# Conditioning rows as whole 2048-wide tiles of 1 MB, and a new share-out of them over the groups of a two-layer trunk

## The chip, the cores and the metric

The kernel runs on one core of one Trainium2 chip. The metric is the device time of one execution in microseconds (us). A core has TensorE (PE, matmuls; PEld is its weight load), VectorE (DVE), ScalarE (ACT), GpSimd (POOL) and SyncE (SP), each with an in-order queue of its own, and 16 DMA engines that move data between HBM and SBUF. Matmul results land in PSUM.

## The reference

A sequence of 256 tokens with 2048 features passes two layers. Each layer is a token mixer followed by a squared-ReLU MLP with 8192 hidden features. Layer 0 mixes with an attention of three branches (compressed, selected, window), layer 1 with differential attention. Every sub-layer is conditioned by a vector `c`: six vectors of 2048 per layer come from one large matrix-vector product, and they scale, shift and gate.

```
mod_all = einsum('bd,lde->lbe', silu(c), ada_w) + ada_b        # 2 layers x 6 vectors x 2048
for i in range(2):
    sh1, sc1, g1, sh2, sc2, g2 = split(mod_all[i], 6)
    h = rms_norm(x, attn_norm_g[i]) * (1 + sc1) + sh1
    x = x + g1 * mixer_i(h)                                    # ends in an output projection 2048 x 2048
    h = rms_norm(x, mlp_norm_g[i]) * (1 + sc2) + sh2
    x = x + g2 * (square(relu(h @ mlp_w1[i])) @ mlp_w2[i])
```

All data are float32. `ada_w` alone is 201 MB, and all weights together some 600 MB, each byte of which is read once.

## The kernel before

**Weight groups.** All large products are done in groups. A group is four steps `u`; each step loads two weight tiles of 128 x 1024 float32 (512 KB, tag `raw`, five buffers) from SyncE's queue, and `split` turns each into a rounded part `wH` (ACT) and the remainder `wL` (DVE), with three buffers each, so that TensorE can use its fp32r format: three matmuls per product (line 239 to 241, or 231 to 233 where the activations are the stationary side). `ws_group` runs a group with weights as the stationary side into two PSUM tiles; four such PSUM tiles exist.

**The conditioning rows.** One conditioning vector is 16 rows of 128 x 2048: 128 outputs on the partitions, 2048 inputs along the row. A row is loaded and multiplied with the broadcast `silu(c)` (`cbc`) in one DVE instruction that also sums it up (`accum_out`). The 32 rows of the first two vectors are done in stage 1 by `ada_row`, whole, beside the first weights (`ws`, tiles `psc`, `psv`). The other 160 rows wait in a list `ada_q` in the order layer 0 vectors 2 to 5, layer 1 vectors 0 to 5. `ada_tile` does one of them as two halves of 1024, 512 KB each, in a pool of three buffers (`ADAB`).

Each step of a group ends in `ada_step(rate)`, which issues rows from the list at a given rate:

```
ada_credit[0] += rate
while ada_credit[0] >= 1.0 - 1e-9 and ada_pos[0] < len(ada_q):
    l, vec, kt = ada_q[ada_pos[0]]
    ada_tile(l, vec, kt)
    ada_pos[0] += 1
    ada_credit[0] -= 1.0
```

`ada_until(l, vec)` issues what is still missing up to a vector, and sets the credit to zero for each row that it forces. `ada_vec` adds the halves and the bias once a vector's 16 rows are traced.

**Order.** The instructions are traced in program order and a scheduler gives each engine a fixed queue before the kernel runs. A conditioning load is kept behind the last weight load traced before it (`issue_after(last_load[0])`), and its DVE instruction has its priority lowered by 150 (`AOFF`). A load waits in SyncE's queue until its buffer is free, with all later loads behind it.

**Stages.** After stage 1 come the key groups k0 and k1 (weights `wi`), whose steps also do a part of the compression MLP (weights `cw1`, tile `hidps`) at rate `RA` = 1.3; four query groups with attention at `RB` = 1.2; the output projection `nwo` at `RC` = 1.6. `w_out_phase` runs the projection's first two column groups to three quarters early, finishes them, and then runs groups 2 and 3. Behind group 2 `ready()` needs vectors 3 and 4, and twelve of the sixteen scalings of the next input `z` follow; behind group 3 the last four. Then `mlp` begins with `pair`: two groups (tiles `m_z`) that run on the unnormalised `z` while the norm's statistics and the modulated input `hn` are still being made; these two have no `ada_step`. Groups nb 2 and nb 3 of chunk 0 run at `CR[2]`, `CR[3]`, the first `w2` group at `CR[4]`, and `ada_until(0, 5)` stands ahead of its `residual`, which needs vector 5. All other MLP groups (108 steps) run at `MR0`. Layer 1 does the same: a pair `dvz`, `dkz`, ten groups dq, dk, dv with attention at `DR`, the projection `dwo` at `DR`, an MLP.

Of the kernel before, what the change touches and what calls it, by code (L numbers as in the profile page):

```python
# [11 lines left out]
F32 = mybir.dt.float32  # L12
# [4 lines left out]
ALU = mybir.AluOpType  # L17
PSUM = bass.MemoryType.PSUM

P = 128  # L20
T = 256
TT = T // P
D = 2048
KT = D // P
DFF = 8192
DEPTH = 2
# [7 lines left out]
AOFF = 150  # L34
PMA = ((0, 1), (0, 2), (1, 1))

RA, RB, RC = 1.3, 1.2, 1.6
DR = 0.3
MR0 = 0.8
MR1 = 0.3  # L40
CR = (0, 0, 1, 1, 1)
NEARLY = 2
ACT_SET = "natural_log_exp_and_others"
DH = 128
# [13 lines left out]
NVEC = 6 * KT  # L58
# [17 lines left out]
def emit(ctx, tc, nc, a):  # L76
# [5 lines left out]
    adap = pool("adap", bufs=ADAB)  # L82
# [3 lines left out]
    sm = pool("sm", bufs=2)  # L86
# [10 lines left out]
    def tt(out, in0, in1, op):  # L97
        V.tensor_tensor(out=out, in0=in0, in1=in1, op=op)  # L98

    def stt(out, in0, scalar, in1, op0, op1, **kw):  # L100
        V.scalar_tensor_tensor(out, in0, scalar, in1, op0=op0, op1=op1, **kw)  # L101
# [10 lines left out]
    def sc(name):  # L112
        return scp.tile([P, 512], F32, tag="sc", name=name)
# [18 lines left out]
    cbc = cst.tile([P, D], F32, name="cbc")  # L132
# [6 lines left out]
    for q in range(4):  # L139
        ps = sc("cps")  # L140
# [6 lines left out]
    adaacc = {}  # L147
    mod = cst.tile([P, DEPTH, 6, KT], F32, name="mod")
    bT = smallT[:, SM_B:SM_B + DEPTH * NVEC].rearrange("p (l v) -> p l v", l=DEPTH)

    last_load = [None]

    def acc_tile(l, vec):
        if (l, vec) not in adaacc:
            adaacc[l, vec] = sm.tile([P, KT, 2], F32, tag="adaacc", name="adaacc", bufs=3)
        return adaacc[l, vec]

    def ada_tile(l, vec, kt):
        e = vec * KT + kt
        for j in range(2):  # L160
            r = adap.tile([P, 1024], F32, tag="ada", name="adaraw")
            if last_load[0] is not None:
                with tc.issue_after(last_load[0]):
                    nc.sync.dma_start(r, a["adaT"][l, e, j])
            else:
                nc.sync.dma_start(r, a["adaT"][l, e, j])
            acc = acc_tile(l, vec)[:, kt, j:j + 1]
            with tc.high_priority(offset=-AOFF if (l, vec) > (0, 1) else 0):
                stt(r, r, 1.0, cbc[:, j * 1024:(j + 1) * 1024], ALU.mult, ALU.mult, accum_out=acc)


    def ada_row(vec, kt):
        r = actp.tile([P, D], F32, tag="act", name="adarow")
        nc.sync.dma_start(r.rearrange("p (j d) -> p j d", j=2),
                          a["adaT"][0, vec * KT + kt].rearrange("j p d -> p j d"))
        acc = acc_tile(0, vec)[:, kt, 0:1]
        stt(r, r, 1.0, cbc, ALU.mult, ALU.mult, accum_out=acc)
        return acc

    def ada_vec(l, vec):  # L180
        e = vec * KT
        m = mod[:, l, vec, :]
        tt(m, acc_tile(l, vec)[:, :, 0], acc_tile(l, vec)[:, :, 1], ALU.add)
        tt(m, m, bT[:, l, e:e + KT], ALU.add)

    ada_q = []
    for l in range(DEPTH):
# [8 lines left out]
    def ada_step(rate):  # L196
# [6 lines that stand above are left out]
            if kt == KT - 1:  # L203
                ada_vec(l, vec)

    def ada_until(l, vec):
        while ada_pos[0] < len(ada_q) and ada_q[ada_pos[0]][:2] <= (l, vec):
            ada_credit[0] = 0.0
            ada_step(1.0)
# [33 lines left out]
    def mm_tile(name):  # L243
        return mmp.tile([P, 512], F32, tag="mm", name=name)

    def xs_group(name, srcs, tiles, rate, extra=None):
        ps = [mm_tile(f"{name}{t}") for t in range(TT)]
        for u in range(4):
            for hf in range(2):
                H, L = split(load(srcs(u)[hf]))  # L250
                for j in range(2):
                    kt = u * 4 + hf * 2 + j
                    for t in range(TT):
                        xs_mm(ps[t], tiles, kt, t, H, L, j * 512, 512, kt == 0, kt == KT - 1)
            ada_step(rate)
            if extra is not None:
                extra(u)
        return ps

    def ws_part(ps, srcs, tiles, rate, us, extra=None):  # L260
        for u in us:
            for hf in range(2):
                H, L = split(load(srcs(u)[hf]))
                for n, j in [(n, j) for n in range(4) for j in range(2)] if u * 2 + hf == 7 else \
                        [(n, j) for j in range(2) for n in range(4)]:
                        kt = u * 4 + hf * 2 + j
                        ws_mm(ps[n // 2][:, (n % 2) * T:(n % 2 + 1) * T], tiles, kt, H, L,
                              j * 512 + n * P, kt == 0 and n % 2 == 0, kt == KT - 1 and n % 2 == 1)
            ada_step(rate)
            if extra is not None:  # L270
                extra(u)

    def ws_group(name, srcs, tiles, rate):
        ps = [mm_tile(f"{name}{t}") for t in range(2)]
        ws_part(ps, srcs, tiles, rate, range(4))
        return ps
# [223 lines left out]
    def residual(tn, ps, nb, l, vec, stats):  # L500
        for n in range(4):
            kt = nb * 4 + n
            stt(xT[:, kt, :], ps[n // 2][:, (n % 2) * T:(n % 2 + 1) * T], mod[:, l, vec, kt:kt + 1],
                xT[:, kt, :], ALU.mult, ALU.add)
            if stats:
                if nb == 3:
                    tn.scale(kt)
                tn.st.add(kt)
        if stats and nb == 2:
            tn.ready()  # L510
            for kt in range(12):
                tn.scale(kt)
# [3 lines left out]
    def pop(more=False):  # L516
        for _ in range(1 + more):
            if pend:
                pend.pop(0)()

    def w_out_phase(name, src, tiles, l, rate, extra=None):
        tn = Turn(l, 1)
        early = [[mm_tile(f"{name}{nb}_{t}") for t in range(2)] for nb in range(NEARLY)]
        for nb in range(NEARLY):
            ws_part(early[nb], lambda u: src[nb, u], tiles, rate, range(3), extra and (lambda u: extra()))
        while pend:
            pop()
        ada_until(l, 2)
        for nb in range(4):
            if nb < NEARLY:  # L530
                ps = early[nb]
                ws_part(ps, lambda u: src[nb, u], tiles, rate, range(3, 4))
            else:
                ps = ws_group(f"{name}{nb}_", lambda u: src[nb, u], tiles, rate)
            residual(tn, ps, nb, l, 2, True)
        return tn

# [69 lines left out]
    for kt in range(KT):  # L607
        acc = ada_row(1, kt)
        stt(Amod[:, 0, 0, kt:kt + 1], acc, b1[:, kt:kt + 1], ag[:, 0, kt:kt + 1], ALU.add, ALU.mult)
        acc = ada_row(0, kt)  # L610
# [4 lines left out]
        f, la = kt == 0, kt == KT - 1  # L615
# [8 lines left out]
    for i in range(2):  # L624
        V.memset(kcT[i][:, :, 256:272], 0.0)
        for b in range(2):
            src = ps_c[i][b].rearrange("p (g t) -> p g t", g=2)
# [93 lines left out]
    def part(i, hp):  # L721
        def f(u):
            cmp_part(i, hp, u)
            pop()
        return f

    hidk = cmp_start(0)
    ps = xs_group("k0_", lambda u: blocks[0, u], h, RA, part(0, hidk))
    pend += [k_block(tab_ks, (128, 0), ps), lambda: cmp_end(0, hidk)]
    hidv = cmp_start(1)  # L730
    ps = xs_group("k1_", lambda u: blocks[1, u], h, RA, part(1, hidv))
# [5 lines left out]
    for g in range(GROUPS):  # L737
        ps = xs_group(f"q{g}_", lambda u: blocks[2 + g, u], h, RB, lambda u: pop())
# [9 lines left out]
        for r in range(4):  # L748
# [3 lines left out]
            for t in range(TT):  # L752
# [21 lines left out]
                for b, src, dst in segs:  # L774
                    act(dst, src, AF.Exp, scale=qss[t][:, 0, r:r + 1], bias=mx[:, b:b + 1],
                        accum_out=su[:, b:b + 1])
# [27 lines left out]
    stn = w_out_phase("nwo", a["nwo"], o, 0, RC)  # L804
    tn = mlp(0, stn, (MR0, CR), False)
    tab_dq = rope_table(ROW_DQ, 0, 2, "tab_dq")
# [7 lines left out]
    for i in range(2):  # L814
        stt(lj, lamb[:, 2 * i, :], 1.0, lamb[:, 2 * i + 1, :], ALU.mult, ALU.mult,
            accum_out=lamt[:, i:i + 1])
# [96 lines left out]
    def diff_k(srcs, kd):  # L913
        st = []

        def norm():
            for t in range(TT):
                st.append(k_norm_rope(srcs[t].rearrange("p (g d) -> p g d", g=4), tab_dk, t, 4, P, krs[t]))

        def flip():  # L920
            for t in range(TT):
                act(kd[:, :, t, :], transpose4(st[t]))

        pend.insert(0, norm)
        pend.append(flip)
# [5 lines left out]
    for g in range(4):  # L931
# [20 lines left out]
        else:  # L952
            diff_k(xs_group(f"dk{g}_", lambda u: a["di"][g * 3 + 1, u], h1, DR, lambda u: pop()), kd)
        ps = xs_group(f"dq{g}_", lambda u: a["di"][g * 3 + 2, u], h1, DR, lambda u: pop())
        diff_q(ps, g, kd, vd)
        if g:
            ps = xs_group(f"dv{g}_", lambda u: a["di"][g * 3, u], h1, DR, lambda u: pop(g == 3))
            for t in range(TT):
                act(vd[:, t, :], ps[t])

    stn = w_out_phase("dwo", a["dwo"], od, 1, DR, pop)
    mlp(1, stn, (MR1, CR), True)
    ada_until(DEPTH - 1, 5)


def c_(v):
    return np.ascontiguousarray(v)
# [73 lines left out]
```

## Time and profile before

| | |
|---|---|
| three runs | 2395.89 us median (2390.55 to 2396.08) |
| profiled execution | 2395.7 us, span 2393.7 us |
| TensorE clock granted, mean | 0.996 of full |
| busy share of the span | PE 98%, PEld 91%, DVE 71%, ACT 48%, POOL 2% |
| moved by DMA | 612.71 MB, 256 GB/s over the span |
| chain that ended last | PE 86%, DVE 6%, DMA 4%, ACT 2% |

A busy share is an average over stages. Matmuls are pipelined and the profile models their ends, so that a matmul of 281 ns in it starts 0.12 us behind the one before; the number of matmuls in a stretch says more than the busy time. A wait is put down to what came last. The granted clock of a stretch lies between 1.2 and 2.4 GHz: 1.00 is the whole stretch at 2.4.

### The profile page before, as it was taken

How to read it: one execution, taken by the hardware profiler on the slowest of the kernel's cores; microseconds unless marked ns; L12 is line 12 of the kernel's file. 1: busy time of each engine (PE TensorE's matmuls, PEld its weight loads, DVE VectorE, ACT ScalarE, POOL GpSimd, SP SyncE). 2: the span in 40 equal slices, each digit the busy share in tenths (PEclk: the TensorE clock that was granted, in tenths of full speed). 3: DMA queues.
4: the chain of work that ended last, by engine and by line, in shares of the span. 5: the costliest groups of instructions: out<-in, count | busy, mean ns of one | idle time of the engine just before them, and what ended most of it. 6: DMA issues, size and time to landing. Idle time of an engine off the chain costs nothing.

```text
span 2393.7 us, 42873 instructions
## 1 busy us (share of the span) xinstructions
PE 2352.3 (98%) x17171; PEld 2189.6 (91%) x17171; DVE 1688.2 (71%) x2594; ACT 1150.2 (48%) x1914; POOL 41.2 (2%) x41
## 2 busy tenths in 40 slices
PE   8998999989999999999999999999999999999999
PEld 5566778989999999999998778799999999999999
DVE  6776999899888887887887765666745445445454
ACT  2133577556435435435456555664643543543443
POOL 0001000000000000000000000100000000000000
PEclk9999999999999999999999999999999999999999
DMA  9988877888898998989986655445555555555554
GB/s 376 414 327 302 300 261 262 284 305 313 328 340 337 339 332 322 341 330 333 328 295 205 208 198 176 156 152 185 180 188 184 180 189 185 184 186 184 185 194 149
DMA packets 168887, 612.71 MB, mean 256 GB/s; under 512 B 18416, under 2 KB 19824, under 8 KB 168688
## 3 DMA queue, kind: packets, MB, share of 16 engines
q1 hardware_dynamic: 167536, 609.06, 72.2%
q8 instruction: 134, 2.20, 0.4%
q10 hardware_dynamic: 1152, 0.92, 0.1%
q14 instruction: 65, 0.53, 0.1%
HBM read 607.81 MB, written 2.10 MB: 255 GB/s over the span
## 4 chain that ended last, share of the span: by engine, by line
PE 86%; DVE 6%; DMA 4%; ACT 2%; issue 1%; POOL 1%; SPq 0%; DVEq 0%; ACTq 0%; POOLq 0%
PE m L241 19%; PE m L239 19%; PE m L240 19%; DMA adaraw<-adaT 2%; DMA adarow<-adaT 2%; DVE wL L98 2%; PE dwo L240 1%; PE dwo L239 1%; PE dwo L241 1%; PE psc L618 1%; DVE adaraw L101 1%; PE m_z L241 1%; PE m_z L240 1%; PE m_z L239 1%; DVE adarow L101 1%
## 5 line engine op out<-in xcount | busy, mean ns | idle before, releaser
L98 DVE TENSOR_TENSOR wL<-raw,wH 128x1024 fp32r<-128x1024 f32 x721 | 880.1, 1223 | 544.8 <-ACT wH L95 541.3
L95 ACT ACTIVATE wH<-raw 128x1024 fp32r<-128x1024 f32 x721 | 762.7, 1059 | 947.5 <-PE m L240 684.7
L240 PE MATMUL m<-hd,wH 128*128 128x256 f32 x2048 | 576.4, 281 | 0.0
L241 PE MATMUL m<-hd,wL 128*128 128x256 f32 x2048 | 576.3, 281 | 0.0
L239 PE MATMUL m<-hd,wH 128*128 128x256 f32 x2048 | 575.9, 281 | 0.0
L239 PE MATMUL m<-hn,wH 128*128 128x256 f32 x1792 | 504.4, 281 | 0.0
L241 PE MATMUL m<-hn,wL 128*128 128x256 f32 x1792 | 504.3, 281 | 0.0
L240 PE MATMUL m<-hn,wH 128*128 128x256 f32 x1792 | 504.1, 281 | 0.0
L101 DVE SCALAR_TENSOR_TENSOR adaraw<-adaraw,cbc 128x1024 f32<-128x1024 f32 x320 | 385.7, 1218 | 16.2 <-DMA adaraw<-adaT 15.9
L241 PEld LDWEIGHTS m<-hd,wL 128*128 128x128 f32 x2048 | 387.2, 189 | 0.0
L240 PEld LDWEIGHTS m<-hd,wH 128*128 128x128 f32 x2048 | 386.5, 189 | 0.0
L239 PEld LDWEIGHTS m<-hd,wH 128*128 128x128 f32 x2048 | 386.4, 189 | 0.0
L241 PEld LDWEIGHTS m<-hn,wL 128*128 128x128 f32 x1792 | 338.6, 189 | 0.0
L240 PEld LDWEIGHTS m<-hn,wH 128*128 128x128 f32 x1792 | 338.6, 189 | 0.0
L239 PEld LDWEIGHTS m<-hn,wH 128*128 128x128 f32 x1792 | 337.9, 189 | 0.2 <-ACT zb L95 0.2
L101 DVE SCALAR_TENSOR_TENSOR adarow<-adarow,cbc 128x2048 f32<-128x2048 f32 x32 | 73.2, 2287 | 14.1 <-DMA adarow<-adaT 14.1
L241 PE MATMUL m_z<-z,wL 128*128 128x258 f32 x256 | 70.9, 285 | 5.7 <-DVE wL L98 5.7
L241 PE MATMUL nwo<-o,wL 128*128 128x256 f32 x256 | 73.1, 286 | 1.5 <-DVE wL L98 1.5
L618 PEld LDWEIGHTS psc<-h,raw 128*128 128x128 f32 x256 | 49.5, 197 | 26.4 <-ACT h L95 17.9
L239 PE MATMUL nwo<-o,wH 128*128 128x256 f32 x256 | 73.3, 286 | 0.0
L239 PE MATMUL m_z<-z,wH 128*128 128x258 f32 x256 | 72.9, 286 | 0.0
L239 PE MATMUL dwo<-od,wH 128*128 128x256 f32 x256 | 72.9, 285 | 0.0
(300 smaller groups left out, 3326.8 us busy)
## 6 DMA issues: line engine op xcount, KB each, us to landing
raw<-w SPq DMA_DIRECT2D x512, 512.0 KB, 4.4
adaraw<-adaT SPq DMA_DIRECT2D x320, 512.0 KB, 5.5
raw<-di SPq DMA_DIRECT2D x96, 512.0 KB, 3.9
adarow<-adaT SPq DMA_DIRECT2D x32, 1024.0 KB, 11.8
raw<-wi SPq DMA_DIRECT2D x48, 512.0 KB, 5.9
raw<-ws SPq DMA_DIRECT2D x32, 512.0 KB, 10.3
raw<-nwo SPq DMA_DIRECT2D x32, 512.0 KB, 4.9
raw<-dwo SPq DMA_DIRECT2D x32, 512.0 KB, 3.4
```

Of the source, the lines that this page charges most:

```text
L95: return S.activation(out=out, in_=in_, func=func, **kw)
L98: V.tensor_tensor(out=out, in0=in0, in1=in1, op=op)
L101: V.scalar_tensor_tensor(out, in0, scalar, in1, op0=op0, op1=op1, **kw)
L239: TE.matmul(ps, H[:, off:off + m], xh, start=first, stop=False)
L240: TE.matmul(ps, H[:, off:off + m], xl, start=False, stop=False)
L241: TE.matmul(ps, L[:, off:off + m], xh, start=False, stop=last)
L618: TE.matmul(ps_c[i][n // 2][:, (n % 2) * T:(n % 2 + 1) * T], wc[:, i * 512 + n * P:i * 512 + (n + 1) * P], full, start=f and n % 2 == 0, s ...
```

## The change

A listed conditioning row becomes one tile of 128 x 2048: one load of 1 MB, one DVE instruction, one sum, and three such buffers in place of three halves. Its place in HBM is laid out so that a partition's 2048 values are contiguous; `ada_row` in stage 1 then needs no rearranged load. `ada_vec` loses the addition of two halves. The scratch that the program sets aside for descriptors made by GpSimd shrinks to 1024 bytes. The last group (nb 3) of both output projections gets the rate 0. The rates `CR` of the three MLP groups behind it go from 1 to 1.2, `MR0` from 0.8 to 0.75, and `DR` of the second layer from 0.3 to 0.35.

```
-DR = 0.3
-MR0 = 0.8
+DR = 0.35
+MR0 = 0.75
 MR1 = 0.3
-CR = (0, 0, 1, 1, 1)
+CR = (0, 0, 1.2, 1.2, 1.2)
...
     def acc_tile(l, vec):
...
-            adaacc[l, vec] = sm.tile([P, KT, 2], F32, tag="adaacc", name="adaacc", bufs=3)
+            adaacc[l, vec] = sm.tile([P, KT], F32, tag="adaacc", name="adaacc", bufs=3)
...
     def ada_tile(l, vec, kt):
-        e = vec * KT + kt
-        for j in range(2):
-            r = adap.tile([P, 1024], F32, tag="ada", name="adaraw")
-            if last_load[0] is not None:
-                with tc.issue_after(last_load[0]):
-                    nc.sync.dma_start(r, a["adaT"][l, e, j])
-            else:
-                nc.sync.dma_start(r, a["adaT"][l, e, j])
-            acc = acc_tile(l, vec)[:, kt, j:j + 1]
-            with tc.high_priority(offset=-AOFF if (l, vec) > (0, 1) else 0):
-                stt(r, r, 1.0, cbc[:, j * 1024:(j + 1) * 1024], ALU.mult, ALU.mult, accum_out=acc)
+        r = adap.tile([P, D], F32, tag="ada", name="adaraw")
+        with tc.issue_after(last_load[0]):
+            nc.sync.dma_start(r, a["adaT"][l, vec * KT + kt])
+        with tc.high_priority(offset=-AOFF):
+            stt(r, r, 1.0, cbc, ALU.mult, ALU.mult, accum_out=acc_tile(l, vec)[:, kt:kt + 1])
...
     def ada_row(vec, kt):
         r = actp.tile([P, D], F32, tag="act", name="adarow")
-        nc.sync.dma_start(r.rearrange("p (j d) -> p j d", j=2),
-                          a["adaT"][0, vec * KT + kt].rearrange("j p d -> p j d"))
-        acc = acc_tile(0, vec)[:, kt, 0:1]
+        nc.sync.dma_start(r, a["adaT"][0, vec * KT + kt])
+        acc = acc_tile(0, vec)[:, kt:kt + 1]
...
     def ada_vec(l, vec):
...
-        tt(m, acc_tile(l, vec)[:, :, 0], acc_tile(l, vec)[:, :, 1], ALU.add)
-        tt(m, m, bT[:, l, e:e + KT], ALU.add)
+        tt(m, acc_tile(l, vec), bT[:, l, e:e + KT], ALU.add)
...
     def w_out_phase(name, src, tiles, l, rate, extra=None):
...
-                ps = ws_group(f"{name}{nb}_", lambda u: src[nb, u], tiles, rate)
+                ps = ws_group(f"{name}{nb}_", lambda u: src[nb, u], tiles, rate if nb < 3 else 0)
...
-    ins["adaT"] = c_(ada_w.transpose(0, 2, 1).reshape(DEPTH, NVEC, P, 2, D // 2).transpose(0, 1, 3, 2, 4))
+    ins["adaT"] = c_(ada_w.transpose(0, 2, 1).reshape(DEPTH, NVEC, P, D))
...
-    nc = bacc.Bacc("TRN2", target_bir_lowering=False, num_devices=1)
+    nc = bacc.Bacc("TRN2", target_bir_lowering=False, num_devices=1, dynamic_dma_scratch_size=1024)
```

## Rows read from the trace of the kernel before

**Rows 1.** The page, busy time of each engine.
```profile
PE 2352.3 (98%) x17171; PEld 2189.6 (91%) x17171; DVE 1688.2 (71%) x2594; ACT 1150.2 (48%) x1914; POOL 41.2 (2%) x41
```

**Rows 2.** Stretches: length; busy PE, PEld, DVE, ACT, POOL; clock; DMA share; GB/s.
```profile
145.00:265.00 120.00, 111.84 (x499) 80.33 (x498) 89.93 (x150) 40.86 (x88) 6.78 (x5) 0.96 0.81 298
265.00:440.00 175.00, 173.49 (x1008) 142.63 (x1007) 162.63 (x457) 133.16 (x401) 8.05 (x8) 1.00 0.77 267
...
530.00:1300.00 770.00, 769.32 (x6422) 767.63 (x6422) 638.15 (x889) 364.69 (x455) 0.00 (x0) 1.00 0.87 319
...
1680.00:2394.00 714.00, 710.03 (x5972) 709.82 (x5970) 360.41 (x372) 319.79 (x366) 0.00 (x0) 1.00 0.56 183
```

**Rows 3.** The same view: the three MLP groups behind the pair.
```profile
560.00:627.00 67.00, 67.00 (x563) 66.84 (x563) 58.94 (x82) 35.07 (x48) 0.00 (x0) 1.00 0.93 343
```

**Rows 4.** The same view in stretches of 10 us, projection's end and pair.
```profile
500.00:510.00 10.00, 9.12 (x74) 8.92 (x75) 9.33 (x18) 5.87 (x10) 0.00 (x0) 1.00 0.88 308
510.00:520.00 10.00, 7.55 (x57) 6.99 (x56) 10.00 (x15) 3.18 (x6) 0.00 (x0) 1.00 0.94 327
...
530.00:540.00 10.00, 10.00 (x73) 10.00 (x73) 9.14 (x16) 3.89 (x7) 0.00 (x0) 0.83 0.59 186
```

**Rows 5.** VectorE in order of time: start, us, line, operation.
```profile
494.38 4.84 DVE L101 SCALAR_TENSOR_TENSOR z<-xT,Amod,z 128x256 fp32r<-128x256 f32 x12
...
515.94 1.22 DVE L101 SCALAR_TENSOR_TENSOR adaraw<-adaraw,cbc 128x1024 f32<-128x1024 f32 x1
...
517.09 1.21 DVE L98 TENSOR_TENSOR wL<-raw,wH 128x1024 fp32r<-128x1024 f32 x1
```

**Rows 6.** What TensorE waited for, 505 to 560 us: total, times, longest.
```profile
PE m_z L241 <- DVE wL L98: 5.7, 3, 2.7
```

**Rows 7.** Stretches of layer 2's attention (columns as in Rows 2).
```profile
1290.00:1425.00 135.00, 131.52 (x633) 106.33 (x632) 92.86 (x153) 76.47 (x178) 12.10 (x10) 1.00 0.64 215
1425.00:1560.00 135.00, 133.34 (x623) 107.31 (x622) 84.52 (x151) 81.21 (x195) 12.65 (x12) 1.00 0.50 164
```

**Rows 8.** The same stretch, conditioning tile alone: length, DVE busy (instructions), clock, DMA.
```profile
1290.00:1425.00 135.00, 16.48 (x27) 1.00 0.64 215
```

**Rows 9.** Groups of VectorE instructions: busy us, mean ns, idle before.
```profile
L101 DVE SCALAR_TENSOR_TENSOR adaraw<-adaraw,cbc 128x1024 f32<-128x1024 f32 x320 | 385.7, 1218 | 16.2 <-DMA adaraw<-adaT 15.9
L101 DVE SCALAR_TENSOR_TENSOR adarow<-adarow,cbc 128x2048 f32<-128x2048 f32 x32 | 73.2, 2287 | 14.1 <-DMA adarow<-adaT 14.1
```

**Rows 10.** SyncE's queue in order of time: when loads are issued.
```profile
164.25 3.33 SPq L164 DMA_DIRECT2D adaraw<-adaT  x3
167.68 0.38 SPq L221 DMA_DIRECT2D raw<-cw  x1
175.61 0.33 SPq L164 DMA_DIRECT2D adaraw<-adaT  x1
...
176.51 0.86 SPq L221 DMA_DIRECT2D raw<-wi  x2
```

**Rows 11.** What TensorE waited for, 172 to 192 us.
```profile
PE k L231 <- ACT wH L95: 1.5, 1, 1.5
PE k L232 <- DVE wL L98: 1.3, 1, 1.3
PE hidps L673 <- DMA raw<-cw: 1.2, 1, 1.2
PE tps L441 <- DVE krn L98: 1.1, 1, 1.1
```

**Rows 12.** Stretches of 10 us behind it (columns as in Rows 2).
```profile
180.00:190.00 10.00, 4.99 (x17) 2.94 (x18) 7.48 (x17) 5.89 (x18) 1.58 (x2) 0.79 0.96 380
190.00:200.00 10.00, 10.00 (x42) 7.02 (x41) 7.20 (x11) 2.12 (x2) 0.00 (x0) 0.86 0.71 239
```

**Rows 13.** Stage 1 from its first matmul on (columns as in Rows 2).
```profile
24.00:145.00 121.00, 115.34 (x388) 74.14 (x387) 93.85 (x141) 19.43 (x39) 0.00 (x0) 0.98 1.00 398
```

**Rows 14.** Tile m_z: operation, count, duration min/median/max, first and last start.
```profile
L239 PE MATMUL m_z<-z,wH x124: 277/282/419, 506.0 to 559.9; 128*128 128x258 f32 x124
```

## The prediction

> **What bounds the kernel now.** I read the page first, then a table of stretches, then in each stretch the engine or queue that keeps TensorE waiting. The page says TensorE is busy 98% [rows 1], but that counts modelled ends, so the table by stage is the better witness [rows 2]. From 530 us to 1300 (first MLP) TensorE is never idle, with VectorE busy 638 of 770 us and the DMA engines 87%; from 1680 on (second MLP) it issues 5972 matmuls in 714 us, 0.1196 us each, with no conditioning rows left. In the first MLP the same matmul costs 67/563 = 0.119 us although conditioning rows run beside it [rows 3]. So nothing that makes those rows cheaper can shorten either MLP; their 1,480 us are TensorE's own. What can move lies before 560 us and in the second layer's attention.
>
> Three places matter there. In 145 to 265 us TensorE is idle 8.2 us [rows 2]. In the output projection's last group and the first two MLP groups behind it (tiles nwo and m_z) VectorE is saturated and TensorE waits for wL [rows 4 to 6]. In 1290 to 1560 us TensorE is idle 5.2 us of 270 [rows 7].
>
> **How many conditioning rows go where.** A step adds its rate to a credit and issues one row of 2048 per whole credit. Counting through the loops: before, the projection's sixteen steps at 1.6 bring the count from 29.6 to 55.2, with 48 needed at `ready`. After, twelve steps bring it to 48.8 and the last four carry none: seven rows (48 to 55) leave the last group. Behind it, MLP groups nb 2, nb 3 and the first w2 group go from 12 rows to 16: credit 0.8 + 8 x 1.2 + 4 x 1.2 makes 63.2, and `ada_until(l, 5)` forces the 64th, with the credit then at zero. The other 108 steps of the MLP carry 81 rows instead of 86, which leaves 15 for layer 2's attention and output projection, where 6.4 remained. The trace agrees for before: about 6.75 rows (27 instructions, four to a row: for each half the product and the read of its accumulator) in 1290 to 1425 [rows 8].
>
> **Part 1, the 1 MB rows on VectorE.** A row costs two halves today and one whole then. The whole one already exists in stage 1: 2287 ns against 2 x 1218 [rows 9]. Instructions overlap a little: in [rows 5] a half occupies the queue from 515.94 to 517.09, 1.15 us, so a row costs 2.30; for the whole I take 2.21 (2287 less the same 0.07 overlap). That saves 0.09 us a row, 14 us over 160 rows. Nearly all of it is hidden behind TensorE (both MLPs). It can show only where VectorE itself sets the pace: 265 to 440 us, where it is busy 163 of 175 us [rows 2] with 25 rows: 2.2 us at most. The opposite bound is the same size, because a 2.2 us instruction can stand in front of a short one that TensorE waits for. I take -1.0.
>
> **Part 2, the deeper buffer.** There are still three buffers, but now for three rows instead of one and a half. SyncE issues in order, so a conditioning load without a free buffer blocks the weight loads behind it. That is visible: steps carry 1.3 rows, and the fourth step carries two, four halves for three buffers. Three halves go at 164.25, one cw load follows, and the fourth half goes only at 175.61, a 7.5 us wait for VectorE; the weights of the next group (wi) follow at 176.51 [rows 10]. TensorE then waits 1.2 us for cw, 1.5 for wH and 1.3 for wL [rows 11], is idle 5.0 us in 180 to 190, and resumes at a granted clock of 0.86 in 190 to 200 [rows 12], that is partly at 1.2 GHz. With three whole buffers both loads find a free one (the rows two and three places earlier were long consumed), so the weights go some 7 us earlier. I take 4.0 us for the three waits and 1.0 for the clock (0.14 of 10 us is 1.4): -5.0. Bounds: 0, if another wait (the k-norm chain through POOL) is as late, and -9.6, the stage's whole idle time with the clock. A loss has a reason too: 1 MB loads sit longer in front of weights; 1 MB at the 398 GB/s of [rows 13] takes 2.6 us, so one exposed load costs +2.6.
>
> **Part 3, the last group without rows.** From 505.9 to 559.9 us the first two MLP groups run, 384 matmuls in 54.0 us [rows 14]. At 0.119 they would take 45.7: 8.3 us are lost. Where: 57 records in 510 to 520 instead of 84, and still 73 in 530 to 540, at a clock of 0.83 [rows 4]. Why: VectorE runs conditioning halves of the last projection group between the wL that TensorE needs [rows 5], and TensorE is seen waiting for wL three times, 5.7 us [rows 6]. The projection's end loses ten records in 500 to 510, 1.2 us [rows 4]. With seven rows gone, 16 us of VectorE work and 7 MB of loads leave just this place. Left there are eight wL, twelve plus four scalings, four residuals: 8 x 1.15 + 20 x 0.40 (twelve scalings in 4.84 us [rows 5]), about 17 us for a group that takes TensorE 22.8 us. So TensorE becomes the bound here. Of 9.5 us I keep 1.5 as staying, for the statistics matmuls between the groups and the twelve scalings in one block: -8.0. Bounds 0 and -9.5.
>
> **Part 4, where the rows go: the three groups from 560 to 627 us.** VectorE: 58.9 us busy before [rows 3] with 12 rows; 4 rows more at 2.21, and 0.09 less for each of the 12, make 66.7 us for 67 us of TensorE. DMA: 24 weight loads of 0.52 MB and 16 rows of 1.05 MB, 29.4 MB. At 398 GB/s [rows 13] that is 73.8 us, 6.8 too many, where before 343 GB/s sufficed [rows 3]. The cover is the stretch in front: with no rows pending, weights run five buffers ahead and three rows are loaded early, 5.6 MB or 14 us of DMA time. If that cover is gone the price is +6.8; I take +1.0. The forced 64th row holds up the first residual, behind which nothing is due until the third w2 group wants its PSUM, 22 us later.
>
> Here a rule of the Trainium skill speaks against the change: "DMA: Bandwidth & Descriptors", section "Where 436 GB/s comes from", puts the HBM side of a core at about 358 GB/s. The trace disagrees for this lone core, with 398 GB/s over 121 us [rows 13]. By the page, as an estimate, the 29.4 MB would need 82 us and the price would be +15, the sum 2399.
>
> **Part 5, layer 2's attention.** It gets 8.6 more rows. Today's 6.75 rows in 1290 to 1425 go with 3.5 us of TensorE idle time; 1425 to 1560, nearly without rows, has 1.7 [rows 7]. The difference, 1.8 us, is 0.27 a row: 8.6 x 0.27 = +2.3. Bounds: 0, because VectorE is busy only 63 to 69% there, and +19, if each row exposes its whole 2.21 us.
>
> **The rest.** Stage 1 loads its 32 rows with 8 KB pieces instead of 4 KB and is near the DMA limit (share 1.00), with 5.7 us of TensorE idle [rows 13]. No row shows such pieces; a gain is at most 5.7, and a loss of 1% on 33.6 MB at 398 GB/s would be 0.8. I take 0. One VectorE addition fewer per vector and the smaller descriptor scratch (no load is issued from POOL) cost nothing.
>
> **Sum**: -1.0 -5.0 -8.0 +1.0 +2.3 = -10.7 us. The profiled execution took 2395.7 us (2.0 outside its span of 2393.7), close to the median of 2395.89. Forecast 2395.7 - 10.7 = 2385.0.
>
> **Rivals.** *A. The stalls stay.* Another wait is as late in both places: the k-norm chain before the second k group, and the scalings and statistics in front of m_z. For: TensorE also waited 1.1 us for krn in the first [rows 11], and that chain runs through ACT. Against: the measured waits are for wL and raw loads. It keeps about half of parts 2 and 3: 2391 to 2394, no measurable change. *B. The DMA binds in the three groups of part 4.* For: 29.4 MB in 67 us is 439 GB/s, above all that the trace shows. Against: the 14 us lead. It costs 6.8 instead of 1.0: 2391; with the page's 358, 2399. *C, on the other side: layer 2 pays each row in full.* A 2.21 us instruction on an in-order VectorE delays wL and the softmax pieces. Price up to 19 instead of 2.3, giving 2402; with part 2 failing as well it passes 2403. It decides from some 1.5 us a row on (8.6 x 1.5 = 13 eats the gain). Against: 0.27 seen today. *D. The gain is larger:* stage 1 and the whole idle time of 145 to 265 go too: 2375.
>
> **Chances.** About 0.3% (7.2 us) is what a measurement can tell from no change, so faster means under 2388.7. Forecast case 0.54, D 0.10, A 0.16, B 0.12, C 0.08. Faster: 0.54 + 0.10 less 0.02 for the forecast's upper edge = 0.62. Same: A, most of B and that edge, 0.29. Slower: C at its full price and the page's form of B with other losses, 0.09. The range 2375 to 2397 takes in D's value, A and B by rows; C is left out. The likeliest case alone spans 2379 to 2390.
>
> **What would show it.** Right: no wait of several us for conditioning buffers in SyncE's queue near 168 us, TensorE not idle in 180 to 190; m_z done in about 46 us with 84 records per 10 us; TensorE never idle from 560 to 627. Wrong: a stall behind a 1 MB load in the w2 group at 605 to 630, wL late in the m groups, or TensorE idle time above 8 us in layer 2's attention.

## The result, and the profile after

The changed kernel took 2412.2 us (median of seven runs, 2403.5 to 2417.1) beside 2394.8 for the kernel before on the same chip: ratio 1.0064, 95% interval 1.0049 to 1.0079. By the medians it is slower by some 17 us; forecast were 2385 with a range of 2375 to 2397, and a chance of 0.09 for slower. Its profiled execution, the one whose trace is read here, took 2403.9 us (span 2401.9), 8.2 above the profiled execution before. It is one of the two fastest of the seven. The other 9 us between the medians are in runs that left no trace.

The table of stretches of the changed kernel (columns as in [rows 2]; the first line is to be read against [rows 13], the second against [rows 2], the third against [rows 14], the fourth against [rows 3], the last two against [rows 7]):

```profile
24.00:145.00 121.00, 116.11 (x392) 74.86 (x391) 94.60 (x143) 20.36 (x39) 0.00 (x0) 0.98 0.99 397
145.00:265.00 120.00, 114.70 (x521) 82.69 (x520) 92.60 (x130) 45.41 (x106) 7.94 (x7) 0.99 0.89 331
506.00:560.00 54.00, 54.00 (x447) 53.79 (x446) 48.22 (x75) 35.69 (x63) 0.00 (x0) 1.00 0.70 247
560.00:627.00 67.00, 62.80 (x510) 62.18 (x509) 56.36 (x56) 29.52 (x34) 0.00 (x0) 0.97 0.91 356
627.00:1290.00 663.00, 656.67 (x5476) 655.65 (x5477) 515.65 (x549) 300.77 (x360) 0.00 (x0) 0.99 0.84 310
1290.00:1425.00 135.00, 133.13 (x665) 109.18 (x665) 96.79 (x145) 77.98 (x177) 10.37 (x10) 1.00 0.64 222
1425.00:1560.00 135.00, 130.46 (x596) 105.06 (x595) 95.32 (x159) 77.25 (x190) 16.68 (x12) 0.99 0.60 208
```

The first three stretches went as forecast or nearly so. From 560 us on it turns: the stretch to 627 us holds 510 matmuls where there were 563 [rows 3], and TensorE, never idle in the first MLP before [rows 2], now is. What it waited for in the MLPs most, from the view of waits over the whole span (total us, times, longest):

```profile
PE m L233 <- DVE wL L98: 9.7, 5, 4.1
```

Tile starts give the account in us. Each entry is the time from the first start of one tile to the first start of the next (in the first line: from the last psv), before and after:

| stage | before | after | difference |
|---|---|---|---|
| key groups (psv to q) | 96.7 | 91.4 | -5.3 |
| queries and projection (q to m_z) | 265.9 | 269.8 | +3.9 |
| the pair (m_z to m<-hn) | 55.7 | 47.7 | -8.0 |
| groups nb 2, nb 3 (m<-hn to m<-hd) | 45.9 | 45.8 | -0.1 |
| rest of the first MLP (m<-hd to dvz) | 640.4 | 656.7 | +16.3 |
| second layer's attention (dq to dwo) | 264.7 | 267.0 | +2.3 |

Two places make up the +16.3. I take the interval between neighbouring matmul starts beyond 0.119 us and sum it: 7.4 us up to 640, 9.0 behind. The sum holds the waits and also what a lower clock costs after them. In the view by 10 us the two places look like this:

```profile
590.00:600.00 10.00, 10.00 (x85) 10.00 (x85) 4.76 (x5) 4.21 (x7) 0.00 (x0) 1.00 1.01 406
600.00:610.00 10.00, 6.71 (x42) 6.29 (x41) 9.93 (x10) 4.02 (x5) 0.00 (x0) 0.83 0.78 288
...
620.00:630.00 10.00, 8.22 (x69) 8.01 (x68) 9.85 (x13) 3.18 (x3) 0.00 (x0) 1.00 1.00 385
...
1220.00:1230.00 10.00, 7.80 (x66) 7.59 (x64) 7.05 (x14) 5.46 (x11) 0.00 (x0) 1.00 0.76 284
1230.00:1240.00 10.00, 8.08 (x48) 8.09 (x49) 7.83 (x10) 1.88 (x3) 0.00 (x0) 0.66 0.65 233
```

**The first place, 595 to 630 us.** SyncE's queue (start, us, line, load, count) shows conditioning rows in pairs:

```profile
594.80 8.69 SPq L161 DMA_DIRECT2D adaraw<-adaT  x2
604.30 1.46 SPq L213 DMA_DIRECT2D raw<-w  x2
608.79 7.37 SPq L161 DMA_DIRECT2D adaraw<-adaT  x2
616.25 3.26 SPq L213 DMA_DIRECT2D raw<-w  x4
```

The second of each pair waits for a free buffer, 8.7 and 7.4 us, and the weight loads stand behind it. That looks like the cause, but TensorE did not wait for those loads. Its two longest waits here:

```profile
604.33 0.39 PE L233 MATMUL m<-hd,wL 128*128 128x256 f32 x1 [2.47 <-DVE wL L98]
...
627.88 0.38 PE L233 MATMUL m<-hd,wL 128*128 128x256 f32 x1 [1.78 <-DVE wL L98]
```

The weight behind the first one had landed at 590.57, ahead of the hold. ScalarE rounded it only at 600.02, behind the hidden tile `hd` of the group before, and in VectorE's queue its wL stood behind `hd` and a conditioning product. At the second wait the wL stood behind two products and the four residuals. ScalarE's line comes first here, the others are VectorE's:

```profile
600.02 2.94 ACT L95 ACTIVATE wH<-raw 128x1024 fp32r<-128x1024 f32 x3
...
599.63 1.29 DVE L98 TENSOR_TENSOR hd<-sq,hd 128x512 fp32r<-128x512 f32 x2 [5.24 <-ACT hd L95]
600.85 2.28 DVE L101 SCALAR_TENSOR_TENSOR adaraw<-adaraw,cbc 128x2048 f32<-128x2048 f32 x1
...
603.06 3.49 DVE L98 TENSOR_TENSOR wL<-raw,wH 128x1024 fp32r<-128x1024 f32 x3
...
622.42 2.29 DVE L101 SCALAR_TENSOR_TENSOR adaraw<-adaraw,cbc 128x2048 f32<-128x2048 f32 x1
...
625.04 1.66 DVE L101 SCALAR_TENSOR_TENSOR xT<-m,mod,xT 128x256 f32<-128x256 f32 x4
626.61 3.49 DVE L98 TENSOR_TENSOR wL<-raw,wH 128x1024 fp32r<-128x1024 f32 x3
```

The weight of the second wait had been held back (it landed at 621.97), but ScalarE had rounded it by 623.14, 2.7 us before TensorE came to it. So in both the order of the queues made the wait.

**The second place, 990 to 1240 us.** VectorE in order of time:

```profile
1223.94 2.29 DVE L101 SCALAR_TENSOR_TENSOR adaraw<-adaraw,cbc 128x2048 f32<-128x2048 f32 x1 [2.95 <-DMA adaraw<-adaT]
...
1226.15 1.26 DVE L101 SCALAR_TENSOR_TENSOR xT<-m,mod,xT 128x256 f32<-128x256 f32 x3
...
1230.65 3.49 DVE L98 TENSOR_TENSOR wL<-raw,wH 128x1024 fp32r<-128x1024 f32 x3
```

and TensorE at the same moment:

```profile
1231.92 0.58 PE L233 MATMUL m<-hd,wL 128*128 128x256 f32 x1 [4.12 <-DVE wL L98]
```

VectorE stands 2.95 us at the head of its queue for a row that has not landed; the residual and three wL are behind it, and TensorE waits 4.12 us for the first of those. Then the granted clock is lower for a while (0.66 in 1230 to 1240). This one stall, with the slower matmuls behind it, is 6.7 of the 9.0 us; three shorter ones, at 1019, 1134 and 1180, make some 2 more. Most late loads cost TensorE nothing: from 560 to 1250 us VectorE waited for them 22 times; before it was 5 times. The view of VectorE's waits in that stretch, after:

```profile
DVE adaraw L101 <- DMA adaraw<-adaT: 28.3, 22, 3.4
```

and before:

```profile
DVE adaraw L101 <- DMA adaraw<-adaT: 2.3, 5, 1.5
```

### The profile page after: what moved, and what is told of

Read it like the earlier page. It is cut to its first block, busy times and chain, and to the rows that moved or that the text cites. A ratio compares the mean times of both kernels' runs of the same rounds, so it can differ in the third digit from the quotient of the medians.

```text
span 2401.9 us, 42038 instructions
## 1 busy us (share of the span) xinstructions
PE 2357.1 (98%) x17171; PEld 2193.4 (91%) x17171; DVE 1670.5 (70%) x2264; ACT 1149.5 (48%) x1914; POOL 42.6 (2%) x41
## 2 busy tenths in 40 slices
DMA packets 141746, 612.65 MB, mean 255 GB/s; under 512 B 15857, under 2 KB 17265, under 8 KB 116977
## 5 line engine op out<-in xcount | busy, mean ns | idle before, releaser
L101 DVE SCALAR_TENSOR_TENSOR adaraw<-adaraw,cbc 128x2048 f32<-128x2048 f32 x160 | 365.2, 2285 | 45.4 <-DMA adaraw<-adaT 45.3
L232 PE MATMUL nwo<-o,wH 128*128 128x256 f32 x256 | 73.3, 287 | 0.0
L231 PE MATMUL nwo<-o,wH 128*128 128x256 f32 x256 | 73.0, 285 | 0.0
```

What stands on the lines that cost most here:

```text
L231: TE.matmul(ps, H[:, off:off + m], xh, start=first, stop=False)
L232: TE.matmul(ps, H[:, off:off + m], xl, start=False, stop=False)
```

## The experiments

All were compared with the kernel before in interleaved runs on one chip per set. The sets ran on different chips, so the ratios, and not the times, compare one set with another. "To 640" and "behind" are the two parts of TensorE's lost time in us between the first m<-hd and the first dvz, as summed above. They and the pair come from one profiled execution per kernel. "Held" is explained further down.

| kernel | ratio, 95% interval | m_z pair | to 640 | behind |
|---|---|---|---|---|
| changed kernel | 1.0064 [1.0049, 1.0079] | 47.7 | 7.4 | 9.0 |
| whole rows only | 0.9966 [0.9953, 0.9978] | 48.5 | 0.0 | 0.1 |
| shares only | 1.0061 [1.0047, 1.0075] | 48.8 | 8.8 | 10.8 |
| six half buffers | 1.0002 [0.9994, 1.0011] | 49.8 | 0.0 | 0.1 |
| small scratch only | 1.0000 [0.9991, 1.0009] | 56.4 | 0.0 | 0.1 |
| whole rows, empty last group | 1.0003 [0.9995, 1.0012] | 47.7 | 11.1 | 0.9 |
| whole rows, CR 1.2 | 0.9978 [0.9970, 0.9987] | 48.9 | 3.5 | 1.2 |
| whole rows, MR0 0.75 | 1.0011 [1.0000, 1.0022] | 48.5 | 0.0 | 11.5 |
| changed kernel, MR0 0.8 | 0.9981 [0.9973, 0.9990] | 47.7 | 8.9 | 0.9 |
| changed kernel, products held | 0.9999 [0.9990, 1.0009] | 47.7 | 3.5 | 0.1 |
| whole rows, products held | 1.0031 [1.0020, 1.0042] | 47.7 | 0.0 | 1.5 |
| whole rows, MR0 0.85 | 1.0011 [1.0003, 1.0020] | 49.3 | 0.0 | 15.7 |
| whole rows, MR0 0.9 | 1.0060 [1.0048, 1.0072] | 48.5 | 0.0 | 26.6 |

**Whole rows or shares?** The first set takes the change apart. The whole rows alone are the changed kernel with the four share edits undone:

```
-DR = 0.35
-MR0 = 0.75
-CR = (0, 0, 1.2, 1.2, 1.2)
+DR = 0.3
+MR0 = 0.8
+CR = (0, 0, 1, 1, 1)
...
-                ps = ws_group(f"{name}{nb}_", lambda u: src[nb, u], tiles, rate if nb < 3 else 0)
+                ps = ws_group(f"{name}{nb}_", lambda u: src[nb, u], tiles, rate)
```

> The changed kernel with the old shares: rates 0.3, 0.8, 1 and 1.6 in the last projection group again; rows stay whole, 1 MB, three buffers. Theory W (whole rows): the loss in the first MLP comes from 1 MB loads that VectorE awaits at the head of its queue with wL behind (28 us of such waits there after, 2 before). Then this kernel keeps the loss: some 16 us between the first m<-hd matmul and dvz, and also the stall at m_z of before (54 us instead of 48), so about 2412 + 6 = 2418, ratio 1.007 to 1.011. Theory S (shares): the loss comes from two rows in one step at rate 1.2 and from the forced 64th row, which block SyncE for 8 and 7 us at 595 and 609. Then the first MLP takes 640 us as before and only the k groups' gain of 5 to 6 us is left: 2389, ratio 0.998.

It took 2386.1 us (2384.5 to 2389.7), the fastest kernel of this study, with the first MLP at 640.4 as before. The shares alone are the kernel before with those four edits made:

> The kernel before with only the new shares: halves of 512 KB, three buffers, rates 0.35, 0.75, 1.2, and none in the last projection group. Theory W: the stall at m_z is gone (48 us instead of 54) and the first MLP stays at its 640 us: about 2394.8 - 7 = 2388, ratio 0.997. Theory S: the first MLP loses some 16 us here too, with fewer buffered bytes rather more: 2404 to 2415, ratio 1.004 to 1.008.

It took 2408.2 us (2405.9 to 2415.1), with the first MLP at 659.9. So the theory that 1 MB rows disturb the MLP fell, and the loss is in the shares. The account that theory S gave for it (SyncE held by row loads) the trace of this kernel bears out in part: TensorE's wait up to 630.53 us is for a weight requested at 623.65, behind 6.85 us of row loads. In the changed kernel it does not hold, as the first place showed. Two controls, the kernel before with six buffers of a half row (which needs the small scratch), and with the small scratch alone:

```
-ADAB, QRB = 3, 2
+ADAB, QRB = 6, 2
...
-    nc = bacc.Bacc("TRN2", target_bir_lowering=False, num_devices=1)
+    nc = bacc.Bacc("TRN2", target_bir_lowering=False, num_devices=1, dynamic_dma_scratch_size=1024)
```

> The kernel before with six half buffers in place of three (and the smaller scratch, so that they fit), old shares. It has the changed kernel's buffered bytes without its 1 MB loads. Theory W: the gain of the k groups (SyncE not held for 7.5 us at 168) without the loss in the MLP: 2389, ratio 0.997 to 0.998. A rival, D (depth): deeper buffers let row loads run ahead of weight loads and are themselves the loss: ratio above 1.003, with waits for wL in the first MLP.

> The kernel before with only the smaller descriptor scratch, which moves tiles in SBUF. Control: all theories expect no change, ratio 0.999 to 1.001.

Both are within 0.1% of the kernel before; for six halves that is the figure of neither theory. They shorten the key groups (94.0 us; 96.7 with the small scratch alone, 91.3 with whole rows) and the pair (49.8), but lose 9.5 us in queries and projection (275.6 against 266.1).

**Which share?** My first reading of the shares' loss, steps with two rows at 595 to 630, could not explain late rows at 1220. A new theory came from the order of the queues. A row's product is its multiplication on VectorE. As its place I count how many weights have been split (wL) ahead of the product in VectorE's queue, less the weights requested (raw) ahead of its load in SyncE's. In 940 to 1040 us this is -0.5 on average over the halves before, -0.9 with whole rows only, -2.3 in the changed kernel: there the product stands 1.4 weights further forward than with whole rows only, or 4 us, one weight being 24 matmuls, 2.86 us of TensorE. The time from a load's landing to its product (median, 940 to 1250 us) is 3.5 us with whole rows only and 0.2 in the changed kernel. So I took the shares one by one, each into the kernel with whole rows and old shares:

```
-... tiles, rate)
+... tiles, rate if nb < 3 else 0)
```

> Whole rows with the old shares, but the last group of the attention output projection carries none. Theory R (the loss is in the lower share of 0.75 alone: with it a row's product is put some two weights earlier in VectorE's queue against its load's place in SyncE's queue, and VectorE waits there for the load with wL behind it): no loss, first MLP (first m<-hd to first dvz) 640 to 642 us, row loads that VectorE waits for in it 0 to 4, total 2384 to 2390. Theory Z (the empty group lets VectorE's backlog drain, and rows come late from there on): first MLP 650 or more, total 2395 or more. Theory C (three shares of 1.2): nothing here, 2386.

2395.4 us: theory R fell as the only cause. The numbers are those that theory Z asked for (first MLP 652.3 us), but its reason is not: there are only two waits for rows in the MLP, and 11.1 us are lost at 619 to 633 alone. SyncE's queue shows why:

```profile
600.48 17.71 SPq L161 DMA_DIRECT2D adaraw<-adaT  x5
618.29 2.17 SPq L213 DMA_DIRECT2D raw<-w  x4
```

and the view by 10 us what it costs:

```profile
620.00:630.00 10.00, 1.48 (x5) 1.19 (x6) 7.92 (x13) 3.17 (x3) 0.00 (x0) 0.62 1.00 407
```

Five rows stand in one run without a weight between them, 17.7 us of SyncE. Counting credits: 48.8 rows at the projection's end and twelve steps at 1 make 60.8, so four of the 64 are forced by `ada_until(0, 5)` behind the step's own row. What the last group no longer carries is owed at that point. Here TensorE does wait for weights that were held back: 6.9 us for wH, while ScalarE waits 13.4 us for the load.

```
-CR = (0, 0, 1, 1, 1)
+CR = (0, 0, 1.2, 1.2, 1.2)
```

> Whole rows with the old shares, but 1.2 in place of 1 in the three groups that carry it. Theory R: no loss in the first MLP, 640 to 642 us, as the 1.2 puts the products no earlier; total 2384 to 2390. Theory C (two rows in one step find the buffer full and hold SyncE for 7 to 9 us with the weights behind them): 5 to 8 us lost at 600 to 630, total 2391 to 2396. Theory Z: 2386.

2389.4 us; 3.5 us are lost up to 640, less than theory C asked for, and not for its reason: from 595 to 630 us no row load holds SyncE for more than 0.7 us. The two waits, at 604.79 and 623.89, are for wL behind a hidden tile with two products and behind the residuals, as in the changed kernel.

```
-MR0 = 0.8
+MR0 = 0.75
```

> Whole rows with the old shares, but 0.75 in place of 0.8 over the MLP. Theory R: the whole loss is here: first MLP 652 to 660 us, 15 to 40 waits of VectorE for row loads in it, total 2398 to 2410. Theories C and Z: no loss, first MLP 640 to 642, total 2385 to 2390.

2397.3 us, by the ratios some 11 more than with whole rows alone; theory R had asked for 2398 or more. Nothing is lost up to 640 and 11.5 us behind, with 32 waits for rows:

```profile
DVE adaraw L101 <- DMA adaraw<-adaT: 44.5, 32, 3.5
```

The product's place is -2.2 in 940 to 1040 here, -0.6 with the empty last group and 0.1 with CR 1.2. So it is the lower share that moves the product, and the two places have different causes. Why the scheduler puts the product there at 0.75 was not examined.

**Is it the place?** The changed kernel with each product held behind the last wL traced before it, which brings its place from -2.3 to 0.0:

```
-        with tc.high_priority(offset=-AOFF):
+        with tc.issue_after(last_split[0]):
             stt(r, r, 1.0, cbc, ...)
...
```

> The changed kernel with all its shares; each row's product is held in VectorE's queue behind the last wL that was asked for before it, so that it can't stand earlier than its step. Theory R: with the place put right the shares cost nothing in the first MLP: 640 to 643 us, waits for row loads below 5, total 2386 to 2396 (some us may be lost elsewhere, where a held product delays a row's buffer). Theory C: 5 to 8 us at 600 to 630 stay, total 2394 to 2402. If it isn't the place but what the shares ask of the DMA queues, the first MLP stays above 652 and the total above 2402.

2393.5 us; the ratio is 0.9999 where the changed kernel has 1.0064, some 16 us less. Behind 640 the loss is 0.1 us, and VectorE's waits show no late row there; 3.5 stay up to 640. The same hold on the kernel with whole rows and old shares:

> Whole rows with the old shares, each row's product held behind the last wL that was asked for before it. It gives the price of the hold by itself, as in the old shares no product is late in the MLP: theory RD: first MLP 640 to 643 us; ahead of the MLP, where buffers come free later, 0 to 4 us lost; total 2385 to 2391. If the hold itself shortened the MLP, the gain of the hold in the changed kernel would prove nothing about the place: then below 2384.

2401.7 us: the hold by itself makes the MLP no shorter (641.8 us against 640.4) and costs 11.3 us ahead of it (q to m_z 281.1 against 269.8; TensorE waits there for wL of the projection), more than the 0 to 4 I had put down. So the gain in the changed kernel comes from the place of the product, as far as one hold can show it: it also takes away the product's lowered priority, and other instructions move with it (at 601.60 us the next group's wL stands ahead of `hd` again).

**Do the two add?** The changed kernel with MR0 back at 0.8:

```
-MR0 = 0.75
+MR0 = 0.8
```

> The changed kernel with 0.8 in place of 0.75 over the MLP; the rest of its shares stay. Theory RD (two causes that add: the lower share of 0.75, some 8 us at 990 to 1240; and the rows that the last group no longer carries, which are owed by the time of the first residual of the MLP and come in steps of two or in a run there, 5 to 8 us at 600 to 630): the second alone is left, first MLP 646 to 650 us, nothing lost behind 640, total 2391 to 2398. Theory R (only the share of 0.75): first MLP 640 to 642, total 2385 to 2389. A third, that the two hang together (late rows only where the others came before): anything above 652.

2391.0 us. Up to 640 it loses 8.9 us, behind 0.9. Of the two places one is left, as the theory of two causes says. Two stretches of this kernel:

```profile
600.00:610.00 10.00, 6.99 (x43) 6.79 (x44) 9.40 (x9) 3.44 (x4) 0.00 (x0) 0.83 0.74 265
...
640.00:1240.00 600.00, 599.56 (x5033) 599.36 (x5032) 481.49 (x494) 270.73 (x310) 0.00 (x0) 1.00 0.89 330
```

**More than 0.8?** If a lower share puts products too early, a higher one should be safe and leave the second layer fewer rows. Whole rows, old shares, MR0 0.85 and 0.9:

```
-MR0 = 0.8
+MR0 = 0.85
```

> Whole rows with the old shares, but 0.85 in place of 0.8 over the MLP. Theory RD: products stand where their loads do or later, first MLP 640 to 641 us; some 5 rows fewer are left for the second layer's attention, which shortens by 1 to 2 us; total 2382 to 2386, a little below the whole rows alone. Rival: 0.85 asks more than VectorE or the DMA queues give in a step, and the first MLP goes above 645, total above 2389.

> As the run with 0.85, with 0.9. Theory RD: first MLP 640 to 642 us, some 10 rows fewer left for the second layer's attention (2 to 4 us shorter there), total 2380 to 2386. Rival: too much for VectorE or the DMA queues in a step, first MLP above 645, total above 2389.

2399.5 and 2409.3 us: a miss. The rival's figures came true, but not its reason: from 640 to 1240 us VectorE is busy 478 us with 0.9 and 481 with 0.8, and the DMA share is 0.87 and 0.88. Behind 640 no product is early (0.0) and no row late, yet the MLP loses 15.7 and 26.6 us. The second layer's attention (dq to dwo) falls to 260.8 and 261.0, but with 0.75, which leaves it more rows, it is 261.0 too. In the view of VectorE's waits from 640 to 1240 us, with 0.9:

```profile
DVE hd L98 <- ACT hd L95: 26.2, 12, 5.2
DVE xT L101 <- PE m L233: 24.0, 14, 2.7
```

With whole rows and 0.8 the first is 7.2 us and the second 2.0. Here VectorE stands at a group's end, for the hidden tile or the residual, with the next group's wL behind:

```profile
740.34 0.69 DVE L98 TENSOR_TENSOR hd<-sq,hd 128x512 fp32r<-128x512 f32 x1 [4.16 <-ACT hd L95]
741.81 1.23 DVE L98 TENSOR_TENSOR wL<-raw,wH 128x1024 fp32r<-128x1024 f32 x1 [0.77 <-ACT wH L95]
```

It is the order of the changed kernel's first place: at 907.80 us this kernel too has `hd` twice after a wait of 5.24 us, a product, and three wL, and TensorE waits. That a fuller plan puts those instructions ahead of wL is my reading of the traces; no run tried it.

## Why the prediction was wrong

**The step that failed** is the one in the first part: "nothing that makes those rows cheaper can shorten either MLP; their 1,480 us are TensorE's own", from which I also took that the other 108 steps, now at 0.75, cost nothing: the sum has no term for them. No run made the first MLP shorter than 640.4 us. But TensorE is never idle there only while each wL is on time, and wL shares VectorE's in-order queue with the rows. A share is an input to the order of that queue. With 0.75 the products stand some 4 us further forward against their loads, and VectorE waits for loads that take about 7 us to land. Fewer rows per step cost 9.0 us in the changed kernel and 11.5 with that one number changed. I priced the work moved, and not the order that is made anew.

**Part 4** was mis-sized: +1.0 forecast; 7.4 lost up to 640 in the changed kernel, 8.9 with MR0 0.8, a little above the upper bound of 6.8. The credits were counted rightly, the forced row too. What failed is "the forced 64th row holds up the first residual, behind which nothing is due": the next weights' wL stand behind that residual in VectorE's queue, and TensorE waits 1.78 us for them. The larger part, 3.3 us of waits at 600 to 604 and the lower clock behind them, is a hidden tile and a row ahead of wL, an order that the sum did not price. With the empty last group alone, and with the shares in halves, TensorE does wait for weights that row loads had held back. Which of the two shares sets the order in the changed kernel was not separated. The price is not DMA bandwidth, as rival B had it: in 600 to 610 us the DMA share is 0.78 with 288 GB/s while TensorE starves, for a weight that had landed 9 us before. What the Trainium skill gives as the HBM side of a core ("DMA: Bandwidth & Descriptors", section "Where 436 GB/s comes from": about 358 GB/s) does not decide here either; 406 GB/s moved in 590 to 600 us with TensorE never idle.

**Part 3** has the right size (-8.0 for -8.0) and is shown by the shares alone (48.8 for 55.7). But the whole rows give it already with a full last group (48.5); the empty group adds 0.8 to that and brings the owed rows with it. I summed it as if it were independent of the buffers.

**Part 2** was right in size, -5.0 for -5.3, with the waits moved as rival A supposed: the k-norm chain is what is left. TensorE's waits from 170 to 192 us after:

```profile
PE tps L433 <- DVE krn L98: 2.2, 1, 2.2
PE k L224 <- DVE wL L98: 0.8, 1, 0.8
```

In 180 to 190 it is idle 3.0 us, not 0 as I had asked for. Six half buffers gave 2.7 us against their control. How much of the gain the depth alone makes stays open: the whole rows with MR0 0.85, the same kernel up to this point, took 94.6 us here where the whole rows alone took 91.3.

**Part 1** has the wrong sign: +3.9 us from q to m_z where I put -1.0, and the same 269.8 with whole rows alone. A row got cheaper as estimated, 2285 ns in the group's mean for two of 1218 [rows 9]. Of the loss the trace explains a part: TensorE is idle 4.2 us there instead of 3.0, of that 2.4 for wL in the projection (1.5 before), and its granted clock is 0.994 instead of 1.00 over the 270 us, by an estimate at most 1.6 us. The rest has no wait of its own in the trace, and its cause stays open.

**Part 5** hit its number, +2.3, by luck. Its price per row is not confirmed: with the same shares in halves the second layer's attention is 0.9 us shorter than before, with 15 rows behind 1250 us where there were 7, and with whole rows it is 261.0 us at 0 rows and at 12 alike. The largest difference between the traces there is one wait: at 1543.9 us TensorE waits 3.7 us for `qs`, a short VectorE instruction, where it waited 1.0 before. Rival C's price did not come.

**The sum.** By stages: -5.3 +3.9 -8.0 -0.1 +16.3 +2.3 = +9.1, and -0.9 from stage 1, make the 8.2 of the two profiled executions. Slower by this much stood in the prediction as C at its full price, or as B with other losses; neither is what happened. Of what I had written to look for if wrong, wL late in the m groups did show; the stalls at 600 to 630 did too, but not behind a 1 MB load in SyncE's queue. That the changed kernel's other runs are up to 13 us above the profiled one stays open.

## What to carry to other kernels

A share or rate that feeds a planner is an edit to the order of every queue, also where it only takes work away: compare, in the trace, the place of a consumer in its engine's queue with the place of its load, before calling an edit free. When rows are taken out of one place, look up the next deadline that collects them, and what stands behind a forced load or product in the same queue. A load that is held in its queue is not yet the cause of a wait: look whether its data had landed before the waiting engine came to it. Measure the parts of a change one at a time: here the new tile alone was 0.3% faster, and the re-tuned shares alone 0.6% slower.

## What the runs showed of the hardware that I had not expected

- Loads with 8 KB per partition in one piece moved no more than those with 4 KB: 397 GB/s in stage 1 after, 398 before [rows 13], with 141,746 DMA packets in the whole kernel for 168,887.
- A stall can cost more than its length. In the changed kernel matmul starts behind the wait of 4.12 us at 1231.9 are 0.21 us apart where they were 0.12, up to about 1237: 2.4 us more, with a granted clock of 0.66 in 1230 to 1240. With the empty last group TensorE lost 7.1 and 2.2 us to two waits between 619.5 and 629.7 and another 1.9 in slower matmuls up to 633; the granted clock of 620 to 630 was 0.62.
- Of four values of the share one is good: in the kernel with whole rows the first MLP lost 11.5, 0.1, 15.7 and 26.6 us at 0.75, 0.8, 0.85 and 0.9, with VectorE no busier at 0.9 than at 0.8.
